# GpSimd instead of VectorE for the low parts of the weight blocks, up to the end of the first token group

## The chip, the core and the metric

The kernel runs on one core of one Trainium2 chip. The metric is the device time of one execution in microseconds (us). The core has a matrix engine (TensorE, PE in the views, with PEld for its weight loads), a vector engine (VectorE, DVE), an activation engine (ScalarE, ACT), GpSimd (POOL) and a queue for plain DMAs (SyncE, SP). They run side by side, each through its own list of instructions in order, and wait for one another through semaphores.

## What is computed

One layer of a diffusion backbone, in float32, for 512 latent tokens of width 1024 and 256 context tokens (batch 1, one layer). The core of the reference, up to the point that matters here:

```python
h = modulate(rms_norm(x, norm1_g[l]), sh1, sc1)
u = h @ w_in[l]                       # queries, keys, conv input, gates
attn_lat = attend_blocked(qn, qr, kn, kr, vv)      # 16 heads
y_a = attn_heads @ w_o_mla
y_c = conformer_conv(u[..., OFF_CONV:OFF_GATE], ...)  # GLU, 31 taps, norm, silu, @ w_pw
g = jax.nn.sigmoid(u[..., OFF_GATE:])
x = x + g1 * ((g[..., :D_MODEL] * y_a + g[..., D_MODEL:] * y_c) @ w_out)
x = x + g2 * peer_ffn(modulate(rms_norm(x, norm2_g[l]), sh2, sc2), ...)
return rms_norm(x, final_g)
```

`peer_ffn` picks 16 of 16384 single-neuron experts per head and token (8 heads) and sums their outputs.

## The kernel before

The 512 tokens are worked in two groups of 256 (`GROUPS`). For the first group, and for the convolution of both, the matmuls run in float32r, which the kernel makes precise by splitting each operand into a high part (the value rounded to float32r) and a low part (the rest, rounded too). `mm3` (lines 123 to 130) then adds three products: high by high (line 128), high by low (line 129), low by high (line 130). For a weight block of 128x1024 the split is done on the core after the load:

- `wload` (line 114) takes a raw buffer (a ring of `RAW` = 3), loads 512 KB into it through SP (line 117), and calls `parts` while `turn["split"]` is set.
- `parts` (line 111) takes two buffers from a ring of `PARTS` = 6, that is, three pairs.
- `two` (line 104) writes the high part with ScalarE (`se.copy`, line 107) and the low part with VectorE (`ve.tensor_sub`, line 108).

The raw buffer comes free when both parts are formed, and SP can then issue the next load into it; loads of the modulation weights (`wm`, line 173) and of the query weights (line 419) use the same ring. A pair comes free when the matmuls of its block are done.

While `turn["split"]` is set for the first time, these stages call `wload`: `conv_in` (eight pieces, two blocks each; a piece's products are gated and then pass 31 taps on VectorE, lines 221 to 228), `query_in` (two blocks), `gate` (two blocks for each of eight chunks, of which four are done ahead beside attention), and `merge` (per chunk one block of `w_o` and one of `w_pw`, then eight blocks of `w_out`). That makes 58 blocks. `conv_norm` (lines 232 to 261) normalises the convolution's output between the first blocks of `merge`; it splits its result with `two` as well, on two tiles. `attention` spreads the conv pieces, the gates ahead and the modulation loads between the heads as fillers. After the first `merge` the flag is cleared (line 990), and the second group's weights are used unsplit. In the last stage, `dense`, the flag is set again and the expert tables go through `split`, `parts` and `two`.

GpSimd's own work in this kernel is to fetch expert rows by indirect DMAs (lines 717, 761, 777) from the middle of the program on, and one of four one-hot products per step in `scatter_gates` (line 836).

The order of each engine's instructions is not the order of writing. The library that builds the program plans it: it plays the program through with costs of its own for each instruction, and puts next on an engine what is ready and was written first. The taps of a conv piece thus stand between instructions of attention.

Of the kernel before, what the change touches and what calls it, by code (L numbers as in the profile page):

```python
# [10 lines left out]
F32R = mybir.dt.float32r  # L11
# [7 lines left out]
P = 128  # L19
D = 1024  # L20
# [21 lines left out]
RAW, PARTS, GPB, PTB, DPARTS = 3, 6, 6, 2, 4  # L42
# [29 lines left out]
def tile_layer(ctx, tc, a, out):  # L72
    nc = tc.nc
    te, ve, se, ge, sy = nc.tensor, nc.vector, nc.scalar, nc.gpsimd, nc.sync
# [3 lines left out]
    wp = ctx.enter_context(tc.tile_pool(name="wp", bufs=1))  # L78
# [14 lines left out]
    def big(name, dt=F32):  # L93
        return k4.tile([P, D], dt, name=name, tag="k4")

    turn = {"split": False, "w": -1}

    def wtile(name):
        turn["w"] = 0 if turn["split"] else (turn["w"] + 1) % (RAW + PARTS)
# [1 line left out]
            return wp.tile([P, D], F32, name=name, tag="w", bufs=RAW)  # L101
        return wp.tile([P, D], F32, name=name, tag="wp", bufs=PARTS)

    def two(raw, alloc):

        h, l = alloc(), alloc()
        se.copy(h, raw)  # L107
        ve.tensor_sub(l, raw, h)  # L108
        return h, l

    def parts(raw):
        return two(raw, lambda: wp.tile([P, D], F32R, name="wp", tag="wp", bufs=PARTS))

    def wload(src, i, k=KC):

        raw = wtile("wt")
        sy.dma_start(raw, src[i])
        return tuple(t.rearrange("p (k c) -> p k c", k=k) for t in (parts(raw) if turn["split"] else (raw,)))
# [113 lines left out]
    def conv_norm(y):  # L232

        raw = [big("sT").rearrange("p (k t) -> p k t", k=4) for _ in range(2)]
        pm = ps2()
        for k in range(KC):
            te.matmul(pm[:, :GT], ones, y[:, k], start=k == 0, stop=k == KC - 1)
        mu = sp.tile([P, GT], F32, name="mu", tag="mu", bufs=2)
        se.mul(mu, pm[:, :GT], 1.0 / D)
        for q in range(2):  # L240
            yv = y[:, 4 * q:4 * q + 4]
            ve.tensor_sub(yv, yv, mu[:, None, :].to_broadcast([P, 4, GT]))
            se.activation(raw[q], yv, AF.Square)
        pv = ps2()
        for k in range(KC):
            te.matmul(pv[:, :GT], ones, raw[k // 4][:, k % 4], start=k == 0, stop=k == KC - 1)
        rd = sp.tile([P, GT], F32, name="rd", tag="mu", bufs=2)
        se.activation(rd, pv[:, :GT], AF.Sqrt, bias=eps_t, scale=1.0 / D)
        ve.reciprocal(rd, rd)
        hi, lo = [], []  # L250
        for q in range(2):
            yv = y[:, 4 * q:4 * q + 4]
            ve.tensor_mul(yv, yv, rd[:, None, :].to_broadcast([P, 4, GT]))
            for j in range(4):
                k = 4 * q + j
                se.activation(yv[:, j] if turn["split"] else raw[q][:, j], yv[:, j], AF.Silu, bias=lnb[:, k:k + 1], scale=lng[:, k:k + 1])
            if turn["split"]:
                h, l = two(yv, lambda: big("sp", F32R).rearrange("p (k t) -> p k t", k=4))
                hi.append(h)
                lo.append(l)  # L260
        return (hi, lo) if turn["split"] else (raw,)
# [22 lines left out]
    with tc.tile_pool(name="tmp0", bufs=1) as t0:  # L284
# [65 lines left out]
        for i in range(6):  # L350
            ps = ps1()
            for k in range(KC):
                l = (hT[i // 2] if i < NT else hcT)[k // 4][:, k % 4, (i % 2) * P:(i % 2 + 1) * P]
# [492 lines left out]
    def split(src, c, name):  # L846
        raw = wtile(name) if name == "u" else big(name)
        sy.dma_start(raw, src[c])
        return parts(raw) if name == "u" else two(raw, lambda: dn.tile([P, D], F32R, name=name, tag="vp", bufs=DPARTS))
# [137 lines left out]
    conv.close()  # L987
    gp = ctx.enter_context(tc.tile_pool(name="gp", bufs=GPB))
    x1 = merge(GROUPS[0], hh, aT, lambda: conv_norm(y), ready=ready[0])
    turn["split"] = False  # L990
    sy.dma_start(hb, hTd)
    y = ep.tile([P, KC, GT], F32, name="y", tag="y")
    sy.dma_start(y, yd)
# [107 lines left out]
```

## Time and profile before

| | us |
|---|---|
| median of 2 runs | 1969.0 (1966.42 and 1971.58) |
| profiled execution | 1971.02 |
| span of that execution in the trace | 1969.2 |
| TensorE busy | 1780.8 |
| VectorE busy | 1556.7 |
| ScalarE busy | 777.2 |
| GpSimd busy | 763.7 |

The span is the time from the first to the last instruction in the trace; the profiled execution is 1.8 us longer. A busy time is the union of an engine's instructions, whatever they do; the ends of matmuls are modelled, so that a busy TensorE is not yet one at its peak.

### The profile page before, as it was taken

The page shows a single profiled execution, that of the slowest core. Times are in us where ns is not written, and L with a number is a line of the kernel's source. Part 1 is how long each engine was busy: PE and PEld are TensorE (multiplying, and loading weights), DVE is VectorE, ACT ScalarE, POOL GpSimd, SP SyncE. Part 2 cuts the span into 40 slices and gives each one's busy share as a digit, 9 for nine tenths or more (in the row PEclk, how much of TensorE's full clock was granted, in tenths as well). Part 3 has the DMA queues.
Part 4 walks back from the last instruction along what each step waited for, and adds up shares of the span by engine and source line. Part 5 has one row for each costly group of instructions (what it writes and reads, how often), then busy time and mean ns, then how long its engine had stood idle before and what let it go on. Part 6 is the DMA issues. An engine that isn't in the chain of part 4 may idle for free.

```text
span 1969.2 us, 29888 instructions
## 1 busy us (share of the span) xinstructions
PE 1780.8 (90%) x10952; PEld 1428.7 (73%) x10952; DVE 1556.7 (79%) x3122; ACT 777.2 (39%) x1148; POOL 763.7 (39%) x582
## 2 busy tenths in 40 slices
PE   4799999799996989699996889999999998999997
PEld 2767777598774766573652568788888787888986
DVE  4658989754599989887787774589896478999998
ACT  5246564553224553002111344334444344444444
POOL 0000000000045766555336882366562245655660
PEclk9899999999997999799999999999999999999999
DMA  8143333357486999799877659899999899999994
GB/s 320 39 142 121 122 118 104 119 184 264 163 310 242 324 344 340 293 409 366 291 268 268 238 218 308 297 394 392 400 388 336 306 348 357 400 400 397 400 399 162
DMA packets 179011, 555.67 MB, mean 282 GB/s; under 512 B 18984, under 2 KB 49192, under 8 KB 178608
## 3 DMA queue, kind: packets, MB, share of 16 engines
q1 hardware_dynamic: 105136, 285.29, 40.3%
q0 software_dynamic: 73728, 268.47, 36.9%
q8 instruction: 86, 1.41, 0.3%
q14 instruction: 61, 0.50, 0.1%
HBM read 533.23 MB, written 20.46 MB: 281 GB/s over the span
## 4 chain that ended last, share of the span: by engine, by line
PE 50%; DVE 18%; DMA 16%; issue 9%; POOL 4%; ACT 2%; SPq 0%; DVEq 0%; POOLq 0%; ACTq 0%
PE ps L129 11%; PE ps L128 11%; PE ps L130 11%; DMA g<-in_u_dram,ei 6%; DMA u<-in_ut_dram 4%; DVE scu L720 4%; DMA g<-in_v_dram,iT 4%; PE ps L485 3%; PE acc L766 2%; POOL ohC L836 2%; PE acc L176 2%; DVE wp L108 2%; PE ps L510 2%; PE ps L126 2%; PE ps L837 1%
## 5 line engine op out<-in xcount | busy, mean ns | idle before, releaser
L717 POOL DMA_INDIRECT g<-in_u_dram,ei x256 | 346.9, 1355 | 759.8 <-DVE tk L650 541.0
L720 DVE SCALAR_TENSOR_TENSOR scu<-g,h 128x1024 bf16<-128x1024 f32 x256 | 312.2, 1219 | 37.5 <-DMA g<-in_u_dram,ei 34.5
L128 PE MATMUL ps<-h2hi,wp 128*128 128x256 f32 x1024 | 290.9, 284 | 0.0
L129 PE MATMUL ps<-h2lo,wp 128*128 128x256 f32 x1024 | 289.6, 283 | 0.0
L130 PE MATMUL ps<-h2hi,wp 128*128 128x256 f32 x1024 | 289.6, 283 | 0.0
L777 POOL DMA_INDIRECT g<-in_v_dram,ei x128 | 205.1, 1602 | 147.1 <-DVE vsum L783 119.8
L107 ACT CAST wp<-u 128x1024 fp32r<-128x1024 f32 x128 | 134.3, 1049 | 288.3 <-DMA u<-in_ut_dram 178.1
L761 POOL DMA_INDIRECT g<-in_v_dram,iT x128 | 133.9, 1046 | 244.9 <-PE acc L766 208.1
L108 DVE TENSOR_TENSOR wp<-u,wp 128x1024 fp32r<-128x1024 f32 x128 | 156.1, 1220 | 91.4 <-ACT wp L107 90.4
L128 PE MATMUL ps<-v,wp 128*128 128x512 f32 x512 | 203.9, 398 | 11.6 <-ACT wp L107 6.1
L129 PE MATMUL ps<-v,wp 128*128 128x512 f32 x512 | 205.4, 401 | 8.1 <-DVE v L108 7.9
L128 PEld LDWEIGHTS ps<-h2hi,wp 128*128 128x128 f32 x1024 | 195.9, 191 | 12.8 <-issue 10.9
L130 PE MATMUL ps<-v,wp 128*128 128x512 f32 x512 | 204.2, 399 | 0.4
L129 PEld LDWEIGHTS ps<-h2lo,wp 128*128 128x128 f32 x1024 | 196.1, 192 | 1.8
L130 PEld LDWEIGHTS ps<-h2hi,wp 128*128 128x128 f32 x1024 | 196.1, 191 | 0.0
L225 DVE SCALAR_TENSOR_TENSOR yo<-glu,cvw,yo 128x512 f32<-128x512 f32 x232 | 172.5, 747 | 4.3 <-ACT yo L223 0.9
L108 DVE TENSOR_TENSOR v<-v 128x1024 fp32r<-128x1024 f32 x128 | 156.1, 1220 | 24.3 <-ACT v L107 24.0
L783 DVE SCALAR_TENSOR_TENSOR vsum<-g,act,vsum 128x1024 f32<-128x1024 f32 x127 | 162.6, 1281 | 0.8
L107 ACT CAST v<-v 128x1024 fp32r<-128x1024 f32 x128 | 132.3, 1044 | 47.9 <-PE ps L129 41.6
L766 PE MATMUL acc<-g,Wz 128*32 128x512 f32 x512 | 101.0, 607 | 23.7 <-DMA g<-in_v_dram,iT 21.4
L129 PEld LDWEIGHTS ps<-v,wp 128*128 128x128 f32 x512 | 98.4, 192 | 31.9 <-DVE v L108 12.6
L128 PEld LDWEIGHTS ps<-v,wp 128*128 128x128 f32 x512 | 98.8, 193 | 31.2 <-ACT wp L107 6.7
(306 smaller groups left out, 3652.0 us busy)
## 6 DMA issues: line engine op xcount, KB each, us to landing
v<-in_v_dram SPq DMA_DIRECT2D x128, 512.0 KB, 8.3
u<-in_ut_dram SPq DMA_DIRECT2D x128, 512.0 KB, 8.0
wm<-in_wmod_dram SPq DMA_DIRECT2D x48, 512.0 KB, 4.5
wt<-in_w_pq_dram SPq DMA_DIRECT2D x32, 512.0 KB, 4.1
Gd<-gb SPq DMA_DIRECT2D x16, 928.0 KB, 4.4
gr<-Gd SPq DMA_DIRECT2D x14, 1024.0 KB, 12.9
wt<-in_w_ga_dram SPq DMA_DIRECT2D x16, 512.0 KB, 4.4
wt<-in_w_gc_dram SPq DMA_DIRECT2D x16, 512.0 KB, 3.7
```

The source lines that it names most:

```text
L107: se.copy(h, raw)
L108: ve.tensor_sub(l, raw, h)
L128: te.matmul(o, w[0], x[0], start=start, stop=False)
L129: te.matmul(o, w[0], x[1], start=False, stop=False)
L130: te.matmul(o, w[1], x[0], start=False, stop=stop)
L225: ve.scalar_tensor_tensor(yo, glu[:, w:w + SEQ], cvw[:, m, w:w + 1], yo, op0=ALU.mult, op1=ALU.add)
L717: ge.indirect_dma_start(out=g, out_offset=None, in_=a["u"], in_offset=bass.IndirectOffsetOnAxis(ap=r["ei"][:, s:s + 1], axis=0))
L720: ve.scalar_tensor_tensor(scr, g, 1.0, r["h2"], op0=ALU.mult, op1=ALU.mult, accum_out=r["act"][:, s:s + 1])
L761: ge.indirect_dma_start(out=g, out_offset=None, in_=a["v"], in_offset=bass.IndirectOffsetOnAxis(ap=r["iT"][:, tk:tk + 1], axis=0))
L766: te.matmul(acc[32 * j:32 * j + 32, 512 * c:512 * c + 512], z[:, j, 31 - i:63 - i], gs[j][:, 512 * c:512 * c + 512], start=i == 0, stop=i ...
L777: ge.indirect_dma_start(out=g, out_offset=None, in_=a["v"], in_offset=bass.IndirectOffsetOnAxis(ap=r["ei"][:, s:s + 1], axis=0))
L783: ve.scalar_tensor_tensor(r["sum"], g, w, r["sum"], op0=ALU.mult, op1=ALU.add)
```

## The change

`turn` gets an entry `low` that names the engine for the low parts; it is GpSimd at the start and VectorE from the end of the first `merge` on. `parts` hands it to `two`. Calls of `two` from elsewhere (`conv_norm`, `dense`) keep VectorE by default, and so do the expert tables, since `low` is VectorE by then. The 58 subtractions of line 108 on weight blocks move to GpSimd; nothing else is added or removed.

```diff
-    turn = {"split": False, "w": -1}
+    turn = {"split": False, "w": -1, "low": ge}
...
-    def two(raw, alloc):
+    def two(raw, alloc, eng=ve):
         h, l = alloc(), alloc()
         se.copy(h, raw)
-        ve.tensor_sub(l, raw, h)
+        eng.tensor_sub(l, raw, h)
         return h, l
     def parts(raw):
-        return two(raw, lambda: wp.tile([P, D], F32R, name="wp", tag="wp", bufs=PARTS))
+
+        return two(raw, lambda: wp.tile([P, D], F32R, name="wp", tag="wp", bufs=PARTS), turn["low"])
...
     x1 = merge(GROUPS[0], hh, aT, lambda: conv_norm(y), ready=ready[0])
-    turn["split"] = False
+    turn.update(split=False, low=ve)
```

## Rows read from the trace of the kernel before

**Rows 1.** The page: busy time of each engine, and the busy share of TensorE, VectorE and GpSimd in 40 equal slices of the span (49.2 us each; 9 is 90% or more).

```profile
PE 1780.8 (90%) x10952; PEld 1428.7 (73%) x10952; DVE 1556.7 (79%) x3122; ACT 777.2 (39%) x1148; POOL 763.7 (39%) x582
...
PE   4799999799996989699996889999999998999997
...
DVE  4658989754599989887787774589896478999998
...
POOL 0000000000045766555336882366562245655660
```

**Rows 2.** Busy time of each engine in stretches of the first 480 us: start and end of the stretch, its length, then busy us and instruction count of PE, PEld, DVE, ACT and POOL, the granted TensorE clock as a share of full speed, the DMA engines' busy share and GB/s.

```profile
0.00:480.00 480.00, 426.90 (x3023) 341.11 (x3024) 340.86 (x544) 238.47 (x367) 0.74 (x6) 0.95 0.45 149
...
125.00:355.00 230.00, 229.87 (x1748) 178.63 (x1746) 198.87 (x302) 127.69 (x201) 0.00 (x0) 1.00 0.37 117
340.00:376.00 36.00, 31.80 (x217) 20.35 (x216) 30.91 (x50) 18.73 (x35) 0.00 (x0) 0.91 0.44 137
376.00:403.00 27.00, 18.05 (x104) 16.51 (x104) 12.68 (x13) 14.29 (x20) 0.00 (x0) 0.81 0.23 72
403.00:480.00 77.00, 77.00 (x581) 73.79 (x580) 43.70 (x51) 34.37 (x40) 0.00 (x0) 1.00 0.67 223
```

**Rows 3.** Groups of instructions in the first 490 us: line, engine, operation, output and inputs, shapes, count, then busy us and mean ns of one, then the engine's idle time before them and what ended it.

```profile
L225 DVE SCALAR_TENSOR_TENSOR yo<-glu,cvw,yo 128x512 f32<-128x512 f32 x232 | 172.5, 747 | 4.3 <-ACT yo L223 0.9
...
L108 DVE TENSOR_TENSOR wp<-wt,wp 128x1024 fp32r<-128x1024 f32 x58 | 70.9, 1222 | 44.1 <-ACT wp L107 43.9
L107 ACT CAST wp<-wt 128x1024 fp32r<-128x1024 f32 x58 | 60.7, 1047 | 59.4 <-PE ps L129 44.8 <-issue 4.7 <-PE ps L130 2.2
```

**Rows 4.** Who waited for whom in the first 490 us, SP's queue: total us, times, longest.

```profile
SPq L117 <- DVE wp L108: 79.5, 32, 6.1
...
SPq L173 <- DVE wp L108: 45.1, 14, 5.1
```

**Rows 5.** The first matmuls of the first conv piece, in order of time: start and length in us, engine, line, operation, output and inputs, shapes, count, and in brackets the idle time before and what ended it.

```profile
45.87 0.58 PE L128 MATMUL ps<-hb,wp 128*128 128x256 f32 x1 [8.17 <-ACT wp L107]
46.25 0.42 PE L129 MATMUL ps<-hl,wp 128*128 128x256 f32 x1
47.17 0.58 PE L130 MATMUL ps<-hb,wp 128*128 128x256 f32 x1 [0.51 <-DVE wp L108]
```

**Rows 6.** Waits of VectorE from 125 to 355 us, and the instructions of line 108 in the same stretch and in 125 to 376 us (count, then min/median/max ns, then first and last start).

```profile
DVE glu L221 <- PE ps L130: 9.6, 4, 3.5
DVE st L487 <- PE ps L485: 8.4, 11, 1.2
DVE wp L108 <- ACT wp L107: 7.3, 9, 5.1
...
L108 DVE TENSOR_TENSOR wp<-wt,wp x21: 1215/1220/1226, 124.1 to 354.7; 128x1024 fp32r<-128x1024 f32 x21
...
L108 DVE TENSOR_TENSOR wp<-wt,wp x23: 1204/1220/1226, 124.1 to 370.4; 128x1024 fp32r<-128x1024 f32 x23
```

**Rows 7.** VectorE in order of time where attention and the last conv piece end.

```profile
368.49 1.22 DVE L108 TENSOR_TENSOR wp<-wt,wp 128x1024 fp32r<-128x1024 f32 x1
369.62 0.75 DVE L225 SCALAR_TENSOR_TENSOR yo<-glu,cvw,yo 128x512 f32<-128x512 f32 x1
370.29 0.16 DVE L503 RECIPROCAL rb<-st 128x2 f32<-128x2 f32 x1
370.36 1.20 DVE L108 TENSOR_TENSOR wp<-wt,wp 128x1024 fp32r<-128x1024 f32 x1
371.48 1.53 DVE L225 SCALAR_TENSOR_TENSOR yo<-glu,cvw,yo 128x512 f32<-128x512 f32 x2
...
375.80 0.48 DVE L227 SCALAR_TENSOR_TENSOR y<-glu,cvw,yo 128x256 f32<-128x256 f32 x1
```

**Rows 8.** Waits of TensorE from 340 to 403 us.

```profile
PE ps L128 <- ACT sp L107: 8.5, 1, 8.5
PE ps L495 <- ACT pr L489: 3.3, 1, 3.3
```

**Rows 9.** The merge stage, 403 to 480 us: line 108's instructions, what ScalarE's line 107 waited for, and how long SP's loads took from issue to landing (min/median/max us).

```profile
L108 DVE TENSOR_TENSOR wp<-wt,wp x27: 1219/1226/1226, 403.8 to 475.9; 128x1024 fp32r<-128x1024 f32 x27
...
  PE ps L129: 37.2, 24
...
DMA to landing us min/median/max: 3.2/3.5/6.5
```

**Rows 10.** What GpSimd runs before 500 us, and the two engines' instructions of line 836 and VectorE's of line 832 in `scatter_gates` (min/median/max ns), with GpSimd's configuration instruction.

```profile
L269 POOL MEMSET Wz<- 128x252 f32 x2 | 0.6, 308 | 0.3 <-POOLq L1091 0.3
...
L1091 POOL MEMSET const-float32-0.0<- 128x1 f32 x1 | 0.1, 100 | 0.2 <-issue 0.2
...
L836 DVE TENSOR_SCALAR ohC<-iota,tT x192: 330/342/947, 1059.6 to 1176.1; 128x128 f32<-128x128 f32 x192
...
L836 POOL TENSOR_SCALAR ohC<-iota,tT x64: 782/1336/1532, 1058.9 to 1175.1; 128x128 f32<-128x128 f32 x64
...
L836 POOLq MODIFY_POOL_CONFIG  x2: 43/43/43, 1058.8 to 1058.8; - x2
...
L832 DVE TENSOR_TENSOR ohA<-iota,tT x64: 674/685/852, 1059.0 to 1175.0; 128x512 f32<-128x512 f32 x64
```

## The prediction

> **What bounds the kernel now.** I read the page first. GpSimd does nothing in the first ten slices, VectorE is at 4 to 9 tenths there, TensorE at 9 or nearly so in seven of them [rows 1]. All 58 subtractions that move lie between 45.9 and 475.9 us, so only the first 480 of the 1969.2 us change directly; the table by stretches [rows 2] tells what limits them. From 125 to 355 us, which is attention with the conv pieces and gates as fillers, TensorE is busy 229.87 of 230 us at a granted clock of 1.00 (2.4 GHz), beside a VectorE at 198.87. From 403 to 480 us, the merge, it is busy 77.00 of 77 us and VectorE only 43.70. Between the two, 340 to 403 us, TensorE idles (36 - 31.80) + (27 - 18.05) = 13.15 us: there the last conv piece's taps end, and the norm of the convolution is a chain of small steps over several engines.
>
> Then who waits. VectorE stands 43.9 us before line 108 until ScalarE has the high part [rows 3], and SP waits 79.5 + 45.1 us for line 108 before it can load again [rows 4]. These look large, but they are waits of engines with time to spare. TensorE, whose time the stage is made of, waits from 340 to 403 us for the split convolution result (8.5 us) and one softmax (3.3 us), and never there for a weight block's low part [rows 8]. Only at the very start does it stand for one, 0.51 us [rows 5].
>
> **What the subtraction costs on GpSimd.** On VectorE one takes 1.22 us, 58 take 70.9 [rows 3]. The trace has none on GpSimd, so I bound it. GpSimd's memset of 128x252 takes 308 ns and one of 128x1 100 ns [rows 10]: (308 - 100) / 251 = 0.83 ns a column for one stream. A subtraction has two inputs and an output. If the three streams take turns, 1024 columns cost 0.1 + 3 x 0.85 = 2.65 us; if they all overlap, 0.95 us, the lower end. The upper end is from line 836, whose product of 128 columns takes GpSimd at least 782 ns [rows 10]; if all of that were per column, eight times as many would cost 6.3 us. I take 2.65 us, since the subtraction streams plain rows as the memset does, while line 836 also reads a scalar of each row, whose cost must be mostly fixed. (The Trainium skill, GPSIMD Engine Reference, section Performance versus the Vector engine, gives 4497 ns for a two-input add of 2048 float32 columns, against 2293 ns on VectorE; by that ratio I would estimate 2.4 us, and the sum below would end 0.3 us lower. No row here shows such an instruction.) GpSimd's configuration instruction, 43 ns before its first one in line 836 [rows 10], may come earlier now; it costs nothing visible there.
>
> **The parts, one by one.** *The first piece.* TensorE waits for the first low part until 47.17 us, because VectorE takes 1.22 us after the cast [rows 5]. With 2.65 us this is 1.4 us later, in a chain that goes on through the key and query steps. Ends: -0.3 us (0.95) and +5.0 us (6.3).
>
> *Attention, 125 to 355 us.* VectorE gives up 21 subtractions, 25.6 us, and 7.3 us in which it stood before them for the cast [rows 6]. TensorE has 0.13 us of idle time in this stretch [rows 2], so none of it is a gain. The cover of the later low part is the distance from cast to use, and three pairs of buffers; blocks are spread over 230 us, 11 us for each of 21, four times the 2.65 us. I take 0. If VectorE's taps are held up by GpSimd, this is where it would cost; that is a rival below, worth up to +17 us.
>
> *The end of attention, 355 to 403 us.* The two subtractions at 368.49 and 370.36 us stand among the last taps on VectorE [rows 7]. The last tap (375.80) releases the norm of the convolution, whose end TensorE awaits [rows 8], and the reciprocal at 370.29 releases the last head. Gone, they give back 1.22 + 1.20 = 2.4 us if what follows moves up with them. Next late is then the norm's own chain, which keeps its two subtractions on VectorE. Ends: -13.2 us, all the idle time, and +4.3 us: three subtractions (354.7, 368.5, 370.4) that each hold VectorE 2.65 instead of 1.22 us.
>
> *The merge, 403 to 480 us.* 27 blocks pass from 403.8 to 475.9 us [rows 9]: 72.1 / 26 = 2.77 us a block, TensorE's pace. GpSimd at 2.65 us just keeps it, with 0.12 us to spare. The delay of 1.4 us also moves each raw buffer's release, and with it SP's next load, behind which the loads of x for the residual and the gate row are queued; a load lands in 3.5 us, and ScalarE casts only when TensorE frees a pair, for which it waits 37.2 / 24 = 1.55 us a block [rows 9]. 1.4 is less than 1.55, so the wait for TensorE is still the last. I take 0. Above 2.77 us a subtraction, GpSimd would set the pace and each 0.1 us would cost 26 x 0.1 = 2.6 us; at 6.3 us it is 26 x 3.5 = 91 us.
>
> *After 480 us* GpSimd is free of subtractions before its first fetch, and `dense` keeps VectorE. I take 0; all that follows moves with the merge's end.
>
> The sum: +1.4 + 0 - 2.4 + 0 = -1.0 us. The profiled execution took 1971.0 us, so 1970.0; the median of the two runs is 2.0 us below the profiled one, so I forecast 1968.0 us, which is no change that can be told.
>
> **Rivals.** *GpSimd holds VectorE up: slower.* Both read the same memory, and it could be that a tap, with two inputs there, can't run while GpSimd subtracts. Then moving the work frees nothing: in 125 to 355 us VectorE would have 198.9 - 25.6 + 21 x 2.65 = 229 us of 230. It would still have to wait for TensorE 9.6 + 8.4 = 18 us there [rows 6], so the stretch grows by some 17 us; with +4.3 us at its end and +1.4 us at the start, this gives 1969.0 + 23 = 1992 us. If half of the subtractions fall beside other work, only the end counts, +5.7, 1975 us. For it: GpSimd's line 836 takes 1336 ns in the median against 782 at least, beside VectorE. Against it: VectorE's line 832, with two inputs in that memory and at the same time, takes 685 ns in the median against 674 at least [rows 10], so there VectorE was not the one that paid. The point from which it decides is where VectorE's time passes the stretch, 2.7 us a subtraction. The Trainium skill (SBUF — State Buffer, section Who interferes with whom) has it as a rule: a VectorE instruction with two SBUF inputs and a GpSimd one that reads SBUF exclude each other for a whole instruction, and the earlier one wins. By that rule this rival would be likelier than I make it; the rows of lines 832 and 836 agree with half of it, the half in which GpSimd waits. Chance 0.22.
>
> *GpSimd is the bound of the merge: slower.* If beside other work it takes 1336 / 342 = 3.9 times VectorE's time, as in line 836 [rows 10], a subtraction costs 4.8 us, and the merge 26 x (4.8 - 2.77) = 53 us more: 2022 us. It decides from 2.77 us on, and is over 2% (39 us) from 4.3 us on. For it: the ratio of the only row that both engines share. Against: that row is short, so its fixed cost weighs. Chance 0.10.
>
> *The whole idle time comes back: faster, but little.* If the taps, freed of subtractions and of waits for casts, run ahead by a piece, the norm's chain lies beside attention: 1.4 - 13.2 = -12 us, 1957 us. More can't be won, as TensorE fills the rest. For it: 33 us less work and waiting on VectorE before 355 us. Against: the last piece's taps begin only when TensorE has its products. Chance 0.12.
>
> *The plan is another one.* The planner prices a subtraction on GpSimd in its own way, and may set a piece or a gate elsewhere. The idle 13 us bound the gain; a conv piece set later costs about as much. Chance 0.06, in the range on either side.
>
> **How the numbers follow.** My forecast, 1962 to 1975 us, has 0.50. I take in the faster rival (1957) and the held-up VectorE (1992), which leaves out GpSimd as the bound, 0.10, and some of the plan's cases and the rivals' edges: 1957 to 1992 us. Two per cent is 39 us, about what a measurement of this kernel can tell from no change. Faster by more than that would need three times the idle time there is, 0.01; slower needs a subtraction of over 4.3 us, 0.09 with a little for both slower rivals together; so 0.90 for the same.
>
> **What would show it.** In the profile after, line 108's row on GpSimd, 58 times, should have a mean near 2.65 us. VectorE's busy time should be 71 us less, near 1486, and GpSimd's near 918 us. TensorE's row of 125 to 355 us should stay full, that of 403 to 480 us too, with ScalarE still waiting for TensorE rather than for GpSimd. The taps of line 225 should keep their 747 ns; at 1 us or more, VectorE is held up. TensorE waiting for line 108 in the merge would show GpSimd as the bound. The forecast is wrong if a subtraction takes over 2.77 us or the taps grow.

## The result and the profile after

The changed kernel takes 1995.0 us (1991.24 and 1998.78) against 1969.0 us: a ratio of 1.0123 with a 95% interval from 1.0091 to 1.0154. It is 26 us slower, less than the 2% that I had called tellable, yet clear by the interval. The forecast of 1968.0 us was wrong, and so was the range, 1957 to 1992 us, by 3 us.

In the trace of after every line from 112 on has a number one higher than before, since a blank line was added: the taps are line 226, the maximum of the scores 488, the exponential 490, the transposes 496, the third product of `mm3` 131. The experiments further down have before's numbers.

The page of after: busy time of each engine, share of the chain that ended last, and two of the costliest groups.

```profile
PE 1785.2 (90%) x10952; PEld 1429.2 (72%) x10952; DVE 1544.1 (78%) x3064; ACT 776.0 (39%) x1148; POOL 902.1 (45%) x640
...
L108 POOL TENSOR_TENSOR wp<-wt,wp 128x1024 fp32r<-128x1024 f32 x58 | 144.4, 2498 | 359.5 <-ACT wp L107 358.6
...
L226 DVE SCALAR_TENSOR_TENSOR yo<-glu,cvw,yo 128x512 f32<-128x512 f32 x232 | 208.2, 898 | 7.3 <-ACT yo L224 2.6
```

The 58 subtractions are on GpSimd at 2.50 us each, close to the 2.65 us that I had taken. But VectorE, freed of 70.9 us [rows 3], is only 12.6 us less busy (1556.7 - 1544.1). The taps have grown from 747 to 898 ns in the mean, 172.5 to 208.2 us, 35.7 us in all. The minimum, median and maximum of the taps and of the moved subtractions (count, then ns, then first and last start) show how:

```profile
L226 DVE SCALAR_TENSOR_TENSOR yo<-glu,cvw,yo x232: 731/752/2794, 63.3 to 397.2; 128x512 f32<-128x512 f32 x116
...
L108 POOL TENSOR_TENSOR wp<-wt,wp x58: 2340/2406/3357, 45.6 to 502.8; 128x1024 fp32r<-128x1024 f32 x58
```

The median tap is nearly as before (752 against 746 ns). Of the 232, 20 take 0.95 to 2.8 us, 34.3 us above their share at 748 ns, and every one of those lies beside a subtraction on GpSimd. Of the 32 taps that lie beside one, the 20 began after it and the other 12, which keep their 0.75 us, before it. Two subtractions in the timeline of GpSimd, 260 to 276 us (start and length; idle time before and what ended it in brackets):

```profile
262.94 2.69 POOL L108 TENSOR_TENSOR wp<-wt,wp 128x1024 fp32r<-128x1024 f32 x1 [10.63 <-ACT wp L107]
270.41 2.73 POOL L108 TENSOR_TENSOR wp<-wt,wp 128x1024 fp32r<-128x1024 f32 x1 [4.77 <-ACT wp L107]
```

and the chain of waits of the same stretch (start, length, what):

```profile
262.66 0.76 DVE yo L226
...
263.45 2.75 DVE yo L226
...
266.22 0.76 DVE yo L226
...
270.16 0.76 DVE yo L226
...
270.94 2.74 DVE yo L226
273.68 0.88 DVE st L488
...
275.93 1.00 ACT pr L490 x2
...
276.97 0.87 PE ps L496 x6
```

The first subtraction runs from 262.94 to 265.63 us, and the tap that began at 263.45 ends some 0.55 us after it; the second held tap ends at 273.68, 0.54 us after its subtraction (273.14). In all 20 cases it is 0.55 to 0.56 us, whether the tap began 0.16 or 1.9 us after the subtraction. So a held tap isn't slow in proportion: it does most of its work only when the subtraction is over. The Trainium skill (SBUF — State Buffer, section Who interferes with whom) says that a VectorE instruction with two SBUF inputs and a GpSimd one that reads SBUF exclude each other; the trace agrees, with 2.75 us instead of 0.75 for the tap, and 2.69 instead of 2.41 us for the subtraction, which had begun while another tap ran.

Right behind the second held tap stand the maximum of a head's scores, its exponential and its transposes: here what holds the tap holds TensorE. The table by stretches (columns as in [rows 2]):

```profile
0.00:480.00 480.00, 405.57 (x2873) 320.47 (x2874) 324.36 (x483) 227.69 (x357) 123.20 (x55) 0.94 0.40 134
125.00:355.00 230.00, 213.01 (x1594) 166.95 (x1593) 193.25 (x256) 115.95 (x184) 50.86 (x20) 0.98 0.33 107
430.00:510.00 80.00, 80.00 (x593) 76.22 (x592) 27.56 (x26) 34.21 (x40) 65.44 (x27) 1.00 0.66 225
```

TensorE, full in attention before, now stands idle 17.0 of 230 us there, while VectorE is no busier than before: 193.25 against 198.87 us. In the merge (third row, which lies some 27 us later than before) TensorE is full. Who waits for whom from 125 to 355 us (total us, times, longest):

```profile
DVE glu L222 <- PE ps L131: 21.7, 4, 9.0
...
PE ps L496 <- ACT pr L490: 9.0, 3, 3.6
...
DVE st L488 <- PE ps L486: 6.0, 8, 1.2
...
PE ps L486 <- ACT KT L468: 4.0, 1, 4.0
...
PE ps L131 <- POOL wp L108: 0.3, 1, 0.3
```

TensorE waits 9.0 us for the exponential, and so for the maximum and the taps before it; for GpSimd's low part it waits 0.3 us. VectorE in turn waits 21.7 + 6.0 = 27.7 us for TensorE, against 9.6 + 8.4 = 18.0 before [rows 6].

Two of the other waits, 4.0 us and one of 1.3, go another way, which the taps don't explain. The first, in order of time (GpSimd, SP, ScalarE twice):

```profile
148.98 2.60 POOL L108 TENSOR_TENSOR wp<-wt,wp 128x1024 fp32r<-128x1024 f32 x1 [14.86 <-ACT wp L107]
```

```profile
151.61 0.33 SPq L118 DMA_DIRECT2D wt<-in_w_ca_dram  x1
```

```profile
155.34 1.05 ACT L107 CAST wp<-wt 128x1024 fp32r<-128x1024 f32 x1 [3.68 <-DMA wt<-in_w_ca_dram]
156.41 0.47 ACT L468 COPY KT<-ps 64x384 f32<-64x384 f32 x1
```

The subtraction ends at 151.58 us and frees its raw buffer; only then does SP issue the next load into it. ScalarE stands 3.68 us before the cast of that block (0.2 us before), and behind the cast in its list stands the copy of a head's keys, for which TensorE waits. (In the plan of before that copy stands ahead of the cast.) The 1.3 us at 270 us come in the same way. So up to 5.2 of the 17.0 us come from raw buffers that are freed later, and 9.0 from the path of the taps.

The rest of the lag is busy time. From the maximum of head 0 to that of head 24, TensorE runs the same matmuls before (first row) and after (second):

```profile
121.50:321.80 200.30, 200.17 (x1516) 156.90 (x1516) 172.00 (x261) 113.70 (x176) 0.00 (x0) 1.00 0.37 116
```

```profile
123.10:345.60 222.50, 205.61 (x1523) 160.02 (x1522) 185.56 (x246) 113.56 (x177) 49.38 (x19) 0.98 0.32 104
```

It takes 22.2 us longer: 16.8 us more idle, and 5.4 us more busy, at a granted clock of 0.98 instead of 1.00. From 150 to 200 us, which has the idle 4.0 us near its start, the clock is 0.93 (1.00 before).

The same instruction's start in two traces gives the lag of the later one. In us, before's start and the lag of after and of two experiments:

| instruction | before | after | merge alone | write only |
|---|---|---|---|---|
| maximum of head 0 | 121.5 | +1.6 | +1.4 | +0.6 |
| maximum of head 8 | 185.1 | +8.8 | +1.0 | +1.0 |
| maximum of head 16 | 255.8 | +17.8 | +1.0 | +2.0 |
| maximum of head 24 | 321.8 | +23.8 | +1.2 | +1.0 |
| maximum of head 31 | 367.0 | +27.8 | +6.2 | +1.3 |
| first product with `w_out` | 461.2 | +26.8 | +6.2 | +2.6 |
| last product with `w_out` | 482.8 | +26.8 | +6.2 | +4.5 |

Nearly all of after's loss arises head by head in attention, and the merge adds none. (The two profiled executions end only 20.1 us apart, since they differ again in late stages that the change doesn't touch; the medians differ by 26.0.)

### The profile page after: what moved, and what is told of

Its sections match the earlier page's. It is cut to its first block, busy times and chain, and to the rows that moved or that the text cites. A ratio compares the mean times of both kernels' runs of the same rounds, so it can differ in the third digit from the quotient of the medians.

```text
span 1989.3 us, 29917 instructions
## 1 busy us (share of the span) xinstructions
PE 1785.2 (90%) x10952; PEld 1429.2 (72%) x10952; DVE 1544.1 (78%) x3064; ACT 776.0 (39%) x1148; POOL 902.1 (45%) x640
## 4 chain that ended last, share of the span: by engine, by line
PE 42%; DVE 18%; DMA 13%; issue 13%; POOL 10%; ACT 2%; SPq 0%; POOLq 0%; DVEq 0%; ACTq 0%
PE ps L131 9%; PE ps L130 9%; PE ps L129 8%; DVE yo L226 5%; DMA g<-in_u_dram,ei 5%; PE ps L127 4%; POOL g L778 4%; POOL g L718 3%; DMA g<-in_v_dram,iT 3%; PE acc L767 3%; POOL ohC L837 2%; DVE scu L721 2%; PE ps L486 2%; DMA g<-in_v_dram,ei 2%; DMA u<-in_ut_dram 1%
## 5 line engine op out<-in xcount | busy, mean ns | idle before, releaser
L718 POOL DMA_INDIRECT g<-in_u_dram,ei x256 | 341.3, 1333 | 282.3 <-DVE scu L721 91.5
L108 POOL TENSOR_TENSOR wp<-wt,wp 128x1024 fp32r<-128x1024 f32 x58 | 144.4, 2498 | 359.5 <-ACT wp L107 358.6
L226 DVE SCALAR_TENSOR_TENSOR yo<-glu,cvw,yo 128x512 f32<-128x512 f32 x232 | 208.2, 898 | 7.3 <-ACT yo L224 2.6
L107 ACT CAST v<-v 128x1024 fp32r<-128x1024 f32 x128 | 132.4, 1044 | 46.0 <-PE ps L130 40.2
```

What stands on the lines that cost most here:

```text
L108: eng.tensor_sub(l, raw, h)
L226: ve.scalar_tensor_tensor(yo, glu[:, w:w + SEQ], cvw[:, m, w:w + 1], yo, op0=ALU.mult, op1=ALU.add)
L718: ge.indirect_dma_start(out=g, out_offset=None, in_=a["u"], in_offset=bass.IndirectOffsetOnAxis(ap=r["ei"][:, s:s + 1], axis=0))
```

## The experiments

Theory A: GpSimd's reading holds the taps, and the taps hold the softmax. Theory B: GpSimd is too slow for the merge. Theory C: GpSimd's low parts come too late, or the plan of the instructions changed for the worse. The ratios are to before on the same chip, whose median is 1974.4 us for the first four (merge alone, attention alone, write only, quarters) and 1969.8 us for the others; they differ from the quotients of the medians by up to 0.002. The diffs are against the changed kernel, the one of the single write against the write-only kernel.

**The change in the merge alone.** VectorE forms the low parts up to the end of attention, GpSimd from there: 32 blocks instead of 58.

```diff
-    turn = {"split": False, "w": -1, "low": ge}
+    turn = {"split": False, "w": -1, "low": ve}
...
-    aT = attention(GROUPS[0], QT, fill)
+    aT = attention(GROUPS[0], QT, fill); turn["low"] = ge
```

> The low parts stay on VectorE until attention has been planned and are GpSimd's from the merge's first block on (32 of 58). Theory A (a GpSimd subtraction holds VectorE's taps, which read two tensors from SBUF): nearly no tap runs beside the merge, so the taps of line 225 keep a mean near 750 ns (898 in the changed kernel), the last score matmul's stage ends as before, and the time is 1969 to 1974 us. Theory B (GpSimd's subtraction, 2.4 us, is too slow or too late for the merge, at 2.77 us a block): the merge itself is longer and the time stays above 1985 us.

Measured: 1977.8 us, ratio 1.0016 (0.9986 to 1.0046). The stretch 125 to 355 us is again as before:

```profile
125.00:355.00 230.00, 229.86 (x1739) 178.64 (x1739) 198.83 (x301) 128.32 (x204) 0.00 (x0) 1.00 0.37 117
```

The time is 4 us above the range that I expected, and not told from before's. From the first to the last product with `w_out` 21.6 us pass, as before. Two subtractions of the merge's first blocks still fall beside the last taps (the first begins at 356.0 us; two taps take 2.1 and 2.3 us), and the last head's maximum comes 6.2 us late. Theory B falls.

**The change up to the end of attention alone.** GpSimd forms 26 low parts, VectorE those of the merge.

```diff
-    aT = attention(GROUPS[0], QT, fill)
+    aT = attention(GROUPS[0], QT, fill); turn["low"] = ve
```

> The other part alone: GpSimd forms the low parts of the blocks before the merge (26 of 58), VectorE those of the merge. Theory A: as slow as the changed kernel, 1988 to 1998 us, with some 20 taps stretched to 2 to 2.8 us. Theory B: 1969 to 1974 us.

Measured: 1993.9 us, ratio 1.008 (1.005 to 1.011). 18 taps are held, 31.5 us above 748 ns each, and the last maximum lags by 21.2 us. So most of the loss belongs to this half: by the medians 19.5 us of some 26.

**GpSimd writes but hardly reads.** It subtracts 8 of 1024 columns and then writes zeros over the other 1016 three times, so that its part takes even longer. The low parts are left out but for those columns, with every instruction that uses them in place.

```diff
-        eng.tensor_sub(l, raw, h)
+        eng.tensor_sub(l, raw, h) if eng is ve else (ge.tensor_sub(l[:, :8], raw[:, :8], h[:, :8]), [ge.memset(l.bitcast(F32)[:, 8:], 0.0) for _ in range(3)])
```

> As the changed kernel, but GpSimd subtracts only the first 8 columns and then writes the other 1016 columns three times with a memset, so that it is about as long at work (2.5 us or more) but reads next to nothing; the low parts are left out (zeros), so the output isn't the reference's. Theory A: it is GpSimd's reading that holds the taps; they keep a mean below 770 ns, and the time is 1960 to 1972 us. Theory C (the order of instructions was planned anew, or the low part is late by 1.2 us): the taps aren't the cause, and the time stays at 1985 to 1998 us.

Measured: 1976.6 us, ratio 1.0002 (0.9979 to 1.0025); the time is above the 1960 to 1972 us that I expected, the ratio where theory A has it. The taps, then GpSimd's two instructions, in the first 500 us:

```profile
L225 DVE SCALAR_TENSOR_TENSOR yo<-glu,cvw,yo x232: 729/752/755, 62.2 to 370.7; 128x512 f32<-128x512 f32 x116
```

```profile
L108 POOL MEMSET wp<- x174: 934/946/962, 32.7 to 483.9; 128x1016 f32 x174
...
L108 POOL TENSOR_TENSOR wp<-wt,wp x58: 194/202/640, 44.9 to 482.8; 128x8 fp32r<-128x8 f32 x58
```

```profile
125.00:355.00 230.00, 228.39 (x1730) 177.57 (x1731) 178.96 (x280) 127.57 (x203) 60.66 (x78) 1.00 0.36 117
```

No tap of 232 is over 755 ns, TensorE has 228.39 us in the stretch (third fence), and the loss is gone. GpSimd takes 0.20 + 3 x 0.95 = 3.0 us a block, longer than in after, and is busy longer in this stretch (60.66 against 50.86 us). VectorE's instructions are in after's order, TensorE's but for two matmuls. VectorE waits 30.8 + 9.4 = 40.2 us for TensorE here, more than in after, and nothing is lost: its freed time has become waiting.

So neither the plan as a whole nor a low part that is finished late is the cause, and this much of theory C falls. What is left is that GpSimd reads, and the run takes away two things with it: the held taps, and the late raw buffers, since GpSimd reads only 8 columns of them. The load that was issued at 151.61 us in after is issued at 148.46 us here, and the 4.0 us of TensorE are 1.6, the most that the plan's order can have cost there. No run keeps one of the two without the other, so that their shares rest on the waits in the traces. For the taps there is one more sign: VectorE passes from one maximum (193.88 us in after) to the one that TensorE awaits at 222.19 us in 28.3 us, and through the same instructions in 23.5 us here; three held taps lie between, 5.3 us above their share. Nor was a GpSimd instruction tried that reads one operand.

The short subtractions show the other direction. Of the 58, 16 take 0.28 to 0.64 us instead of 0.20; each of them began while a VectorE instruction with two operands in SBUF ran, and each ends 0.06 us before that one. The one that began first is not held, on either engine.

In the merge, where 3.0 us is over TensorE's pace of 2.77, the lag grows from 2.6 to 4.5 us.

**The same with one write.** This asks what VectorE's freedom is worth when GpSimd neither holds it nor is late; the diff is against the kernel just shown.

```diff
-[ge.memset(l.bitcast(F32)[:, 8:], 0.0) for _ in range(3)]
+[ge.memset(l.bitcast(F32)[:, 8:], 0.0) for _ in range(1)]
```

> As the changed kernel, but GpSimd subtracts 8 columns and writes the other 1016 once with a memset, about 1.15 us in all; the low parts are left out (zeros). It shows the most that VectorE's freedom from all 58 subtractions can bring, with nothing held. If VectorE's time were worth something in these 480 us, the time would be 10 us or more below before; by my forecast's reading (TensorE bounds attention and merge, 2.4 us at the end of attention) it is 0 to 6 us below.

Measured: 1967.3 us, ratio 0.9989 (0.9972 to 1.0007), a gain of some 2 us, not told from none. VectorE is busy 177.14 us in the stretch, 21.7 less than before, and it buys next to nothing. So forming the low parts elsewhere could hardly have won more than the 5 us at the interval's end, as the instructions are planned here.

**Four subtractions of 256 columns.** If a tap must wait for a whole GpSimd instruction, shorter ones should hold it less.

```diff
-        eng.tensor_sub(l, raw, h)
+        [eng.tensor_sub(l[:, c:c + 256], raw[:, c:c + 256], h[:, c:c + 256]) for c in range(0, D, 256)] if eng is ge else eng.tensor_sub(l, raw, h)
```

> As the changed kernel, with each subtraction on GpSimd cut into four of 256 columns. Theory A, each instruction holds a tap for its own length: no tap is over 1.6 us, but three or four times as many are stretched, so that the sum over the taps stays near 208 us (172.5 before); the maxima of the softmax wait for one short piece instead of a whole subtraction, and the time falls to between 1975 and 1990 us. Theory C: as the changed kernel, 1990 to 1998 us.

Measured: 1999.5 us, ratio 1.0108 (1.0067 to 1.0149). I missed the time and the sum.

```profile
L225 DVE SCALAR_TENSOR_TENSOR yo<-glu,cvw,yo x232: 729/752/1282, 60.5 to 392.8; 128x512 f32<-128x512 f32 x116
```

```profile
L108 POOL TENSOR_TENSOR wp<-wt,wp x232: 722/753/1714, 45.6 to 506.9; 128x256 fp32r<-128x256 f32 x116
```

No tap is over 1.28 us now, but 62 of them are stretched, 21.8 us in all; a quarter beside taps takes 1.08 us in the mean, a block 4.3 us. Taps and quarters take turns. The held time fell from 34.3 to 21.8 us and the loss stayed, since the other way has grown. From head 0 to head 24 TensorE is idle 17.4 us, as in after. But only 5.1 us of it are waits for an exponential (9.0 in after), and 10.7 us stand behind three casts that waited 5.3, 5.2 and 3.5 us for a load (5.2 us behind two casts in after). The row of the first:

```profile
153.38 1.05 ACT L107 CAST wp<-wt 128x1024 fp32r<-128x1024 f32 x1 [5.28 <-DMA wt<-in_w_ca_dram]
```

SP issued each of these loads when the fourth quarter of a block had ended, 3.7 to 4.5 us after its first had begun. ScalarE also waits 9.9 us for GpSimd's release of buffers, all of it in the merge, where the products with `w_out` take 25.3 instead of 21.6 us.

**Each low part before the merge formed twice.** Twice the reading, the merge on VectorE.

```diff
-        eng.tensor_sub(l, raw, h)
+        [eng.tensor_sub(l, raw, h) for _ in range(2 if eng is ge else 1)]
...
-    aT = attention(GROUPS[0], QT, fill)
+    aT = attention(GROUPS[0], QT, fill); turn["low"] = ve
```

> GpSimd forms each low part of the 26 blocks before the merge twice, one after the other, into the same place; VectorE those of the merge. Theory A (each subtraction on GpSimd holds one tap for most of its length): 36 to 42 stretched taps instead of 18, their excess near 63 us instead of 32, and the time twice as far above before as with one, 2.0 to 2.6% (2010 to 2025 us). If the loss were a fixed price of the move (another plan, a load of code, the first call), the time would stay at 1990 to 2000 us.

Measured: 2031.2 us, ratio 1.031 (1.029 to 1.0331), more than I expected. 37 taps are held, 66.6 us above their share (31.5 with one subtraction), and the last maximum lags by 59.8 us, nearly three times as much. Here TensorE does wait for GpSimd too, over the first 500 us:

```profile
PE ps L130 <- POOL wp L108: 13.6, 5, 3.3
```

So the held time doubles as theory A has it, but the loss grows by more, and the hold isn't alone in it: from head 0 to head 24, 7.7 us of TensorE's idle time are such waits, another 10.5 us stand behind casts that waited for late loads, and the granted clock is 0.92 (0.98 in after).

**Each low part in the merge formed twice.** This prices the second rival: 4.8 us a block.

```diff
-    turn = {"split": False, "w": -1, "low": ge}
+    turn = {"split": False, "w": -1, "low": ve}
...
-        eng.tensor_sub(l, raw, h)
+        [eng.tensor_sub(l, raw, h) for _ in range(2 if eng is ge else 1)]
...
-    aT = attention(GROUPS[0], QT, fill)
+    aT = attention(GROUPS[0], QT, fill); turn["low"] = ge
```

> GpSimd forms the low parts of the merge alone, each twice, VectorE those before. This is the price of the prediction's second rival: 4.8 us for a block against TensorE's 2.77. If GpSimd then sets the pace, some 26 blocks cost 2.0 us more each, 53 us: 2020 to 2030 us. If the loads or buffers gave more slack than I read, less than 20 us.

Measured: 2035.2 us, ratio 1.0324 (1.0298 to 1.0351). Waits of TensorE from 340 to 560 us:

```profile
PE ps L130 <- POOL wp L108: 26.6, 18, 2.0
PE ps L129 <- POOL wp L108: 13.0, 8, 2.0
```

TensorE waits 26 times, 39.6 us in all, and its granted clock is 0.91 from 400 to 545 us, where after has 1.00 in its merge. From the last maximum to the last product with `w_out` the lag grows from 1.0 to 62.8 us, more than the 53 us of the rival's sum; I can place the 39.6 us. How the rest, 22 us, is made up, with the lower clock and a merge that began beside the last taps, isn't worked out. In after, at half the price, it doesn't wait there: the rival was real, but its point lies between 2.4 and 4.8 us, and the write-only kernel's 3.0 us, with its small growth, puts it near the 2.77 us of the prediction. The attention stretch is as before (229.84 us).

**The change again**, on the chip of the last three.

> The changed kernel itself, once more, with as many rounds as the others, to set them against: 1.0 to 1.5% above before on the same chip (1988 to 1999 us).

Measured: 1995.1 us, ratio 1.0116 (1.0092 to 1.014), with 20 held taps and 34.6 us above their share.

## Why the prediction was wrong, point by point

*GpSimd's price was right.* I took 2.65 us between 0.95 and 6.3; the median is 2.41, and 2.60 us in the mean beside taps. The Trainium skill's ratio (GPSIMD Engine Reference, section Performance versus the Vector engine), which I had worked out to 2.4 us, was nearer.

*The start was right:* +1.4 us forecast; the first matmul with a low part begins 0.85 us late (48.02 us), VectorE's first gating product 1.7 us. GpSimd's configuration instruction costs nothing visible, as taken.

*The merge was right:* from 2.77 us a block on GpSimd would decide, at 2.4 us it doesn't, and TensorE stays full.

*The end of attention was wrong in sign:* -2.4 us forecast. From the seventh to the eighth conv piece no more is lost, but from there to the first product with `w_out` the lag grows from 23.1 to 26.8 us, +3.7. The upper bound there, +4.3 us, was for subtractions that hold VectorE. Without any hold the term comes out: in the kernel with one write the first product with `w_out` is 2.7 us earlier than before.

*Attention was the step that failed.* I wrote "I take 0", since the cover of a later low part is four times its length. That asks after the low part alone, whose lateness indeed costs next to nothing (0.3 us in after). Two other things were put at nothing. The first is the hold: a tap that begins beside a subtraction waits until it is over, and 9.0 of TensorE's 17.0 idle us stand behind it. The second is the raw buffer, whose later release I had worked out for the merge and not for attention: 5.2 us stand behind two casts that waited for a load. An average of 11 us a block says nothing of the block whose buffer SP waits for. And TensorE's busy time grew by some 5 us at the lower clock. I had the hold as the first rival, at 1992 us with a chance of 0.22, and it is the larger part of what happened, at 1995. I argued it down by line 832 of `scatter_gates`, 685 ns beside GpSimd's line 836 [rows 10]: "there VectorE was not the one that paid". That row was read too far. GpSimd's instruction there reads 128 columns, and it was the one that paid, 1336 against 782 ns. All 47 of GpSimd's instructions there that take over 1 us lie beside one of line 832, so the two do collide; and line 832's longest, 852 ns [rows 10], began 0.20 us after one of GpSimd's and ended 0.18 us after it, so VectorE pays there too when it comes second. The median hid this. Here a held tap takes 1.7 us more in the mean (34.3 / 20), and a GpSimd subtraction beside taps 0.2 us more than 2.4.

*The rival's own sum came out right for a wrong reason.* It let VectorE fill up, 229 of 230 us busy, and the stretch grow by 17 us. TensorE did lose 17.0 us in 125 to 355 us, but VectorE is at 193.25 us; and the point from which it should decide, 2.7 us a subtraction, was not reached (2.60 us beside taps). Before attention's end the change takes 26 x 1.22 = 31.7 us from VectorE and gives it 31.5 (the held taps of the kernel changed up to there): its work is the same, and yet the last maximum comes 21.2 us late. The held taps lie in the chain of taps, maximum, exponential and transposes, and the time that VectorE gains lies where it then waits for TensorE. Per us of held tap the last maximum came later by 0.67 us (21.2 / 31.5, the change up to attention's end), 0.90 (59.8 / 66.6, formed twice) and 1.07 (23.4 / 21.8, quarters): no fixed price, as the late loads and the clock are in it. That the engine's fixed order is what keeps the gained time from paying for the held time is my reading of the chain; no run changed that order. One planned with the hold's price in it was not tried.

*Signs named beforehand.* VectorE's busy time should have been 1486 us and is 1544.1; the taps grew; both were named as what would show the forecast wrong. The 0.90 for no change within 2% holds by the ratio, but the range was too short by 3 us: its upper end was the rival's own time, with nothing for that rival's error.

## What to carry to other kernels

Before moving work to GpSimd, list which VectorE instructions beside it read two operands from SBUF, and what follows them in order: if one stands ahead of a softmax step or a matmul, what waits for it can pay nearly the whole length of the GpSimd instruction. Ask also what the slower instruction keeps from being released: here a raw buffer, its next load, and what stands behind the cast on ScalarE. Work taken from an engine is worth only what waits for that engine: 21.7 us of VectorE's time bought some 2 us here, not told from none. In the collisions seen here the engine that came second paid, for up to the length of the other's instruction; if one engine pays in a row, price the other one too.

## What the runs showed of the hardware

The hold isn't limited to the taps. In the merge, the small two-input steps of the gate that took 418 to 425 ns before take up to 2.1 us in the mean after (groups of VectorE from 400 to 560 us):

```profile
L581 DVE TENSOR_TENSOR mT<-sgm,mT 128x256 fp32r<-128x256 f32 x4 | 8.3, 2066 | 1.9 <-ACT mT L580 1.9
L581 DVE TENSOR_TENSOR mT<-sg,mT 128x256 fp32r<-128x256 f32 x4 | 6.7, 1665 | 1.9 <-ACT mT L580 1.9
L578 DVE TENSOR_TENSOR sg<-sg 128x256 f32<-128x256 f32 x4 | 4.7, 1169 | 0.1
L576 DVE TENSOR_TENSOR sgm<-ps,sgm 128x512 f32<-128x512 f32 x4 | 2.8, 691 | 29.7 <-PE ps L131 29.7
```

Line 576, which reads one operand from PSUM, stays at 691 ns (692 before). The lines above it cost 14.6 us more of VectorE, and nothing of the time, as TensorE never waits for them there: the same hold costs all or nothing by what follows it. And GpSimd's price per column is plain: 0.20 us for 8 columns, 0.75 for 256, 2.41 for 1024, (2.41 - 0.20) / 1016 = 2.2 ns a column, against 0.95 us for a memset of 1016.
